# Attention scores of a hybrid decoder layer: products of 128, 64 and 3 rows, and the same with 128 rows throughout

## The chip, the cores and the metric

The kernel runs on one core of a Trainium2 chip. A core has a matrix engine (TensorE, PE in the profile), two engines for element-wise work (VectorE, DVE; ScalarE, ACT), GpSimd (POOL), which here issues the gathering DMAs, and SyncE (SP), which issues the other DMAs. The metric is the device time of one execution in microseconds (us), the median of several runs.

## What is computed

One layer over 1024 tokens of width 1024, in float32. The first half of the mixing width is retention, the second is differential attention with four heads; an expert layer follows. What the change touches is the attention score: each head has two maps of 64 query and key dimensions, and the output takes the first softmax less `lam` times the second.

```python
def diff_attention(q, k, v, lam):            # q,k: (B,T,H,2,d) with d = 64
    qb = (q * (d ** -0.5)).reshape(B, N, C, H, 2, d).transpose(1, 0, 3, 4, 2, 5)
    ...
    def block(args):
        qi, start = args
        ...
        bias = jnp.where(dist >= 0, -slopes[:, None, None] * dist, NEG_INF)
        s = jnp.einsum('bhpid,bhpjd->bhpij', qi, kt) + bias[None, :, None]
        p = jax.nn.softmax(s, axis=-1)
        a = p[:, :, 0] - lam * p[:, :, 1]
        return jnp.einsum('bhij,bhjv->bhiv', a, vt)
```

## The kernel before

Tokens go in eight tiles of 128. Three tiles are the sparse group (their experts are gathered row by row with indirect DMAs), five are the dense group (all experts are computed for them). `front` is a generator that yields the steps of the layer for one group; `weave` mixes the steps of two generators. The written order is not the final one: the framework orders the instructions of each engine by its own model of their times, and what a tile's room (its tag with `bufs` buffers) allows.

Numbers of high precision are kept as a high part, rounded to the fast float32r format, and a low part, the rest. A projection is three products (high by high, high by low, low by high), written in `mm` and shown in the profile as L160, L161, L162. `proj_t` makes a transposed projection into the bank `psT`; for the dense group in two halves of 320 tokens, for the sparse group in one of 384. Its bank has one room.

`att_proj(h)` prepares head h. The projection is evacuated into `pt` (one room). Of the queries, map m has a tile `q2[m]`: its own 64 rows hold the high part (L301, ScalarE), the other 64 rows the low part (L302, VectorE). Of the keys, `kd[m]` holds the high part twice (L316, L317), and `kl` holds the low parts of both maps (L318), so that one 128-row product of `q2[m]` and `kd[m]` gives high by high plus low by high, and a 64-row product of the high queries and `kl` adds high by low. The queries have two rooms per map, `kd` alternates between two places, `kl` has one room (`KL = 1`). The sparse group stores its keys in DRAM (`kd_d`), and the dense group loads them on GpSimd's queue (L309).

`attention(h)` takes the query tiles in turn. For each map and each 512 keys it starts with the linear bias, a product of 3 rows in bfloat16 (L342), adds the 128-row product (L344) and the 64-row product (L345), and in the block on the diagonal a mask (L347). VectorE takes the maximum (L350, L352), ScalarE the exponential (L356), VectorE the weighted difference (L361), TensorE transposes it (L368, `psA`) and multiplies it by the values (L372, `pov`). The steps of head h's attention are woven with its retention (`ret`, L272 to L283) and with the projections of head h + 1.

In the dense group's attention the gathered experts of the sparse tiles are already under way: GpSimd issues the gathers (L860), and VectorE forms their dot products (L862); `gated` opens the way for a fixed number of them after each step. After the attention come the output projection, the routing, the weight matrices of the dense tiles and the long loop over all experts.

Of the kernel before, what the change touches and what calls it, by code (L numbers as in the profile page):

```python
# [13 lines left out]
F32 = mybir.dt.float32  # L14
F32R = mybir.dt.float32r
# [8 lines left out]
P = 128  # L24
# [26 lines left out]
KL = 1  # L51
# [48 lines left out]
def layer_kernel(ctx, tc, x, wt, wn, wo, wq, sk, ut, u, v, gmix, gffn, gfin, gsub, dlam, consts, alb, out):  # L100
# [6 lines left out]
    kd_d = tc.dram_tile([H, 3, P, T], F32, name="kd_d")  # L107
# [25 lines left out]
    def front(m, pp, cst, g0, nt, dense, late):  # L133
        """Steps of the layer up to the routing for tiles g0..g0+nt, in the rooms m."""
# [13 lines left out]
        def chunk(src, shape):  # L148
            """Weights [128, k, m] in their hi and lo parts."""
# [48 lines left out]
        def split_t(src_of, name):  # L198
            """Transposes natural [128 t, 1024] tiles into [128, DC, n] operands."""
# [15 lines left out]
        # input norm  # L215
# [16 lines left out]
        # natural projections: rv, dv, rg  # L232
# [32 lines left out]
        def retention(h):  # L265
            qT, kT = ops[h][:2]
            for t in range(nt):
# [20 lines left out]
                jk = ap.tile([P, P], BF, tag="jk", bufs=2, name="jk")  # L288
# [5 lines left out]
        def att_proj(h):  # L294
            q2 = [ap.tile([P, n], F32R, tag=f"q2{m}", bufs=2, name=f"q2{m}") for m in range(2)]
            for a, b, ps in proj_t(wt[8 + 2 * h], hx):
                pt = ap.tile([P, b - a], F32, tag="pt", name="pt")
                A.activation(pt, ps, AF.Copy, scale=0.125)
                for m in range(2):
                    own, oth = slice(64 * m, 64 * m + 64), slice(64 - 64 * m, 128 - 64 * m)  # L300
                    A.activation(q2[m][own, a:b], pt[own], AF.Copy)  # L301
                    V.tensor_sub(q2[m][oth, a:b], pt[own], q2[m][own, a:b].bitcast(F32))  # L302
            yield
            kd2 = ap.tile([P, 2, L], F32R, tag="kd", name="kd") if h % 2 else fp.tile([P, 2, L], F32R, tag="R", name="kd")
            kd = [kd2[:, m] for m in range(2)]
            kl = ap.tile([P, L], F32R, tag="kl", bufs=KL, name="kl")
            if not first:
                for m, tl in enumerate(kd + [kl]):
                    G.dma_start(tl[:, :lo0], kd_d[h, m][:, :lo0])  # L309
            for a, b, ps in proj_t(wt[8 + 2 * h + 1], hx):  # L310
# [3 lines left out]
                for m in range(2):  # L314
                    own, oth = slice(64 * m, 64 * m + 64), slice(64 - 64 * m, 128 - 64 * m)
                    A.activation(kd[m][own, sl], pt[own], AF.Copy)  # L316
                    A.activation(kd[m][oth, sl], pt[own], AF.Copy)  # L317
                    V.tensor_sub(kl[own, sl], pt[own], kd[m][own, sl].bitcast(F32))  # L318
            if not last:
                for m, tl in enumerate(kd + [kl]):  # L320
                    SY.dma_start(kd_d[h, m][:, lo0:L], tl[:, lo0:].bitcast(F32))
            ops[h] += [q2, kd, kl]
            yield

        def attention(h):
            q2, kd, kl = ops[h][2:]
            dvh = ap.tile([P, g0 + nt, P], F32, tag="dvh", bufs=1, name="dvh")
            SY.dma_start(dvh, dv_d[:g0 + nt, :, h * P:(h + 1) * P].rearrange("t p c -> p t c"))
            for t in range(nt):
# [4 lines left out]
                for m in range(2):  # L334
                    pr = slice(m * 64, (m + 1) * 64)
                    ps = bankA("psS") if both is None else both[:, m:m + 1]
                    ql = slice(t * P, (t + 1) * P)
                    for b in range((Lq + 511) // 512):
# [5 lines left out]
                        PE.matmul(o, q2[m][:, ql], kd[m][:, c0:c1], start=False, stop=False)  # L344
                        PE.matmul(o, q2[m][pr, ql], kl[pr, c0:c1], start=False, stop=not diag)  # L345
# [27 lines left out]
                jk = ap.tile([P, P], BF, tag="jk", bufs=2, name="jk")  # L373
# [25 lines left out]
        # output projection and residual  # L399
# [34 lines left out]
        for hp in range(2 * PH):  # L434
# [4 lines left out]
            skt = fp.tile([P, NK], F32, tag="skt", bufs=1, name="skt")  # L439
# [33 lines left out]
    class Routed:  # L473
        """What the routing of a group leaves for later: key ranks and scores."""
# [8 lines left out]
    def decode(rp, late, t, eqs=("eq", 1), tmp=("tmp", 1), cs=("c2", 1)):  # L483
        """Key indices i1, i2 of tile t as [token, (head, rank)]."""
# [34 lines left out]
    def gates_of(rp, late, nt, tag):  # L519
        """Softmax of the scores of tiles 0..nt, in their place."""  # L520
# [9 lines left out]
    def sparse_routes(rp, late, g0, nt, *rooms):  # L530
        """Steps that leave expert indices and weights of the sparse tiles."""
# [9 lines left out]
    def dense_routes(rp, gp, pp, late):  # L541
        """Steps that put the weight matrices of the dense tiles into DRAM."""
# [22 lines left out]
    def build_g(gp, pp, r, lo, tb):  # L565
        """Weight matrices of one token tile: G[i2, i1, token] into DRAM."""
# [35 lines left out]
    def front_consts(cst, fp, wp):  # L602
# [47 lines left out]
    def weave(a, b, na=1, nb=1):  # L650
        """Steps of a and b in turn, nb of b to na of a."""
# [257 lines left out]
```

## Time and profile before

| what | value |
|---|---|
| time, median of 3 runs | 2943.44 us (2942.09 to 2951.27) |
| span of the profiled execution, its own time on the core | 2961.6 us |
| TensorE busy | 2799.5 us, 95% |
| VectorE busy | 2355.3 us, 80% |
| ScalarE busy | 1064.6 us, 36% |
| GpSimd busy | 1056.9 us, 36% |
| mean granted clock of TensorE over the span | 0.958 |

The profile gives the profiled execution's time only as its span, from the first to the last instruction; it is 18.2 us above the median of the three runs. Matmuls are pipelined: the duration of one reaches into the next, so what a product costs in a stream is read from the distance between two starts. The granted clock is 1.00 at 2.4 GHz and 0.50 at 1.2 GHz; a mean between them is a share of time at each.

### The profile page before, as it was taken

Reading aid. Unit: us, or ns where it says so; the run is one execution under the profiler, and the core shown is the slowest. Engines: PE = TensorE matmul, PEld = TensorE weight load, DVE = VectorE, ACT = ScalarE, POOL = GpSimd, SP = SyncE. Lnnn points to the kernel's source line nnn. Section 1 sums busy time; section 2 is a strip of 40 time slices with the busy share of each in tenths; the row PEclk is TensorE's granted clock in tenths of the full one; section 3 lists DMA queues with packets and bytes.
Section 4 is the critical chain, followed back from the end, with each engine's and each line's share of the span. In section 5 each row is a group of like instructions: output and inputs, shape, how many; then the busy total and the mean of one; then the engine's idle time right before and its main releaser. Section 6 shows DMA issues by size and latency. Waiting matters only on the chain.

```text
span 2961.6 us, 43054 instructions
## 1 busy us (share of the span) xinstructions
PE 2799.5 (95%) x16043; PEld 2478.4 (84%) x16043; DVE 2355.3 (80%) x4522; ACT 1064.6 (36%) x1882; POOL 1056.9 (36%) x786
## 2 busy tenths in 40 slices
PE   7989989998889999999989999999999999999998
PEld 6868877776679999998777788899989989999987
DVE  3455888756769999985777888888889988888988
ACT  4553334433333248996212222222322222222222
POOL 0000003423330000001545444566566666665554
PEclk9989998876989999999999999999999999999999
DMA  5334236744662226667888888899999999999997
GB/s 166 108 121 140 94 118 206 247 150 152 241 239 89 85 97 226 242 240 285 305 293 305 308 301 312 318 330 334 344 337 336 341 341 335 341 338 321 344 339 264
DMA packets 293956, 742.90 MB, mean 251 GB/s; under 512 B 23529, under 2 KB 118761, under 8 KB 293746
## 3 DMA queue, kind: packets, MB, share of 16 engines
q0 software_dynamic: 112320, 405.06, 38.8%
q1 hardware_dynamic: 181426, 335.09, 33.0%
q8 instruction: 125, 2.05, 0.3%
q14 instruction: 85, 0.70, 0.1%
HBM read 670.92 MB, written 69.14 MB: 250 GB/s over the span
## 4 chain that ended last, share of the span: by engine, by line
PE 35%; issue 27%; DMA 11%; DVE 9%; POOL 4%; ACT 1%; POOLq 0%; DVEq 0%; ACTq 0%
DMA gt<-g_d 5%; PE psH L722 4%; PE psH L721 4%; PE psH L720 4%; POOL vg L867 3%; DMA vg<-in_v,idx 3%; PE psV L794 3%; PE psV L795 3%; PE psV L796 3%; DMA gl<-hs_d 2%; DVE sa L869 2%; PE kp L795 2%; PE kp L794 2%; PE kp L796 2%; DVE vl L818 1%
## 5 line engine op out<-in xcount | busy, mean ns | idle before, releaser
L867 POOL DMA_INDIRECT vg<-in_v,idx x384 | 528.5, 1376 | 923.0 <-DVE ug L862 521.5
L860 POOL DMA_INDIRECT ug<-in_u,idx x384 | 520.9, 1356 | 522.1 <-DVE ug L862 370.7
L869 DVE SCALAR_TENSOR_TENSOR sa<-vg,shs,sa 128x1024 f32<-128x1024 f32 x384 | 492.4, 1282 | 42.3 <-DMA vg<-in_v,idx 38.7
L862 DVE SCALAR_TENSOR_TENSOR ug<-ug,sx 128x1024 f32<-128x1024 f32 x384 | 461.2, 1222 | 62.6 <-DMA ug<-in_u,idx 61.9
L720 PE MATMUL psH<-nh,uh 128*128 128x320 f32 x1424 | 439.7, 309 | 0.1
L721 PE MATMUL psH<-nl,uh 128*128 128x320 f32 x1424 | 439.6, 309 | 0.0
L722 PE MATMUL psH<-nh,ul 128*128 128x320 f32 x1424 | 438.7, 309 | 0.8 <-DVE ul L708 0.8
L794 PE MATMUL psV<-vh,wh 128*128 128x512 f32 x768 | 306.8, 401 | 36.3 <-DVE acc L830 35.8
L795 PE MATMUL psV<-vl,wh 128*128 128x512 f32 x768 | 305.0, 398 | 0.0
L796 PE MATMUL psV<-vh,wl 128*128 128x512 f32 x768 | 297.4, 396 | 0.0
L720 PEld LDWEIGHTS psH<-nh,uh 128*128 128x128 f32 x1424 | 267.5, 188 | 6.4 <-ACT uh L706 0.9
L721 PEld LDWEIGHTS psH<-nl,uh 128*128 128x128 f32 x1424 | 267.3, 188 | 5.2
L722 PEld LDWEIGHTS psH<-nh,ul 128*128 128x128 f32 x1424 | 267.1, 188 | 4.4 <-DVE ul L708 1.6
L723 ACT ACTIVATE ga<-psH 128x320 f32<-128x320 f32 x178 | 74.6, 426 | 438.4 <-PE psH L722 396.4
L706 ACT ACTIVATE uh<-uraw 128x1024 fp32r<-128x1024 f32 x128 | 135.7, 1060 | 209.7 <-PE psH L721 120.3
L794 PEld LDWEIGHTS psV<-vh,wh 128*128 128x128 f32 x768 | 147.9, 193 | 68.7 <-DVE acc L830 38.6
L720 PE MATMUL psHs<-nh,uh 128*128 128x320 f32 x624 | 196.3, 316 | 9.1 <-ACT ga L723 8.9
L153 ACT ACTIVATE whi<-wraw 128x1024 fp32r<-128x1024 f32 x104 | 110.1, 1059 | 258.4 <-PE psT L161 141.4
L155 DVE TENSOR_TENSOR wlo<-wraw,whi 128x1024 fp32r<-128x1024 f32 x104 | 126.9, 1220 | 94.6 <-ACT whi L153 92.3
L795 PE MATMUL kp<-vl,wh 128*128 128x512 f32 x512 | 199.2, 392 | 0.4 <-DVE vl L818 0.4
L794 PE MATMUL kp<-vh,wh 128*128 128x512 f32 x512 | 193.2, 393 | 4.7 <-ACT wh L810 4.7
L708 DVE TENSOR_TENSOR ul<-uraw,uh 128x1024 fp32r<-128x1024 f32 x128 | 156.4, 1222 | 48.7 <-ACT uh L706 48.6
(242 smaller groups left out, 6271.0 us busy)
## 6 DMA issues: line engine op xcount, KB each, us to landing
uraw<-in_ut SPq DMA_DIRECT2D x128, 512.0 KB, 6.3
vraw<-in_v SPq DMA_DIRECT2D x128, 512.0 KB, 6.9
g_d<-st SPq DMA_DIRECT2D x80, 512.0 KB, 4.7
gt<-g_d SPq DMA_DIRECT2D x32, 1280.0 KB, 18.0
wraw<-in_wt SPq DMA_DIRECT2D x32, 512.0 KB, 3.7
wraw<-in_wq SPq DMA_DIRECT2D x32, 512.0 KB, 3.8
hs_d<-ga SPq DMA_DIRECT2D x39, 320.0 KB, 2.6
gl<-hs_d SPq DMA_DIRECT2D x39, 320.0 KB, 5.9
```

What stands on the lines that cost most here:

```text
L706: A.activation(uh, raw, AF.Copy)
L708: V.tensor_sub(ul, raw, uh.bitcast(F32))
L720: PE.matmul(ps, uh[:, dc], xh[:, dc, sl], start=(dc == 0), stop=False)
L721: PE.matmul(ps, uh[:, dc], xl[:, dc, sl], start=False, stop=False)
L722: PE.matmul(ps, ul[:, dc], xh[:, dc, sl], start=False, stop=(dc == DC - 1))
L794: PE.matmul(ps, Wh[e][:, sl], Vh[e][:, so], start=start, stop=False)
L795: PE.matmul(ps, Wh[e][:, sl], Vl[e][:, so], start=False, stop=False)
L796: PE.matmul(ps, Wl[e][:, sl], Vh[e][:, so], start=False, stop=stop)
L860: G.indirect_dma_start(out=ug, out_offset=None, in_=u, in_offset=bass.IndirectOffsetOnAxis(ap=idxA[t][:, k:k + 1], axis=0))
L862: gate(V.scalar_tensor_tensor(ug, ug, 1.0, xt, op0=ALU.mult, op1=ALU.mult, accum_out=hs[:, k:k + 1]))
L867: G.indirect_dma_start(out=vg, out_offset=None, in_=v, in_offset=bass.IndirectOffsetOnAxis(ap=idxA[t][:, k:k + 1], axis=0))
L869: gate(V.scalar_tensor_tensor(ac, vg, hs[:, k:k + 1], ac, op0=ALU.mult, op1=ALU.add))
```

## The change

The keys become the operand with two halves, and the queries come twice. `kk[m]` holds the high part of map m's keys in the map's own 64 rows and the low part in the other 64. `qa[m]` holds the high part of the queries in both halves, `qb[m]` the low part in both halves. The product of `qa[m]` and `kk[m]` is high by high plus high by low, that of `qb[m]` and `kk[m]` low by high plus low by low; both have 128 rows. The bias operands have 128 rows, of which 125 are zero. `kl` is gone. Of the rooms, `qb` has one per map, the scratch tile `jk` one instead of two; `skt` and `cd` of the routing share the tags of other tiles and have two. In the profile of the changed kernel the lines after `UG` stand one or two away.

```diff
-KL = 1
...
-    kd_d = tc.dram_tile([H, 3, P, T], F32, name="kd_d")
+    kd_d = tc.dram_tile([H, 2, P, T], F32, name="kd_d")
...
-            q2 = [ap.tile([P, n], F32R, tag=f"q2{m}", bufs=2, name=f"q2{m}") for m in range(2)]
+            qa = [ap.tile([P, n], F32R, tag=f"q2{m}", bufs=2, name=f"qa{m}") for m in range(2)]
+            qb = [ap.tile([P, n], F32R, tag=f"qb{m}", bufs=1, name=f"qb{m}") for m in range(2)]
...
-                    A.activation(q2[m][own, a:b], pt[own], AF.Copy)
-                    V.tensor_sub(q2[m][oth, a:b], pt[own], q2[m][own, a:b].bitcast(F32))
+                    A.activation(qa[m][own, a:b], pt[own], AF.Copy)
+                    A.activation(qa[m][oth, a:b], pt[own], AF.Copy)
+                    V.tensor_sub(qb[m][own, a:b], pt[own], qa[m][own, a:b].bitcast(F32))
+                    V.tensor_sub(qb[m][oth, a:b], pt[own], qa[m][own, a:b].bitcast(F32))
...
-                    A.activation(kd[m][own, sl], pt[own], AF.Copy)
-                    A.activation(kd[m][oth, sl], pt[own], AF.Copy)
-                    V.tensor_sub(kl[own, sl], pt[own], kd[m][own, sl].bitcast(F32))
+                    A.activation(kk[m][own, sl], pt[own], AF.Copy)
+                    V.tensor_sub(kk[m][oth, sl], pt[own], kk[m][own, sl].bitcast(F32))
...
-                        PE.matmul(o, q2[m][:, ql], kd[m][:, c0:c1], start=False, stop=False)
-                        PE.matmul(o, q2[m][pr, ql], kl[pr, c0:c1], start=False, stop=not diag)
+                        PE.matmul(o, qa[m][:, ql], kk[m][:, c0:c1], start=False, stop=False)
+                        PE.matmul(o, qb[m][:, ql], kk[m][:, c0:c1], start=False, stop=not diag)
...
-            skt = fp.tile([P, NK], F32, tag="skt", bufs=1, name="skt")
+            skt = fp.tile([P, NK], F32, tag="at", bufs=2, name="skt")
...
-                cd = fp.tile([P, nt, NC2], F32, tag="kl", bufs=KL, name="cd")
+                cd = fp.tile([P, nt, NC2], F32, tag="q20", bufs=2, name="cd")
...
-        ab = fp.tile([3, H * P + T], BF, tag="ab", name="ab")
+        ab = fp.tile([P, H * P + T], BF, tag="ab", name="ab")
+        V.memset(ab, 0.0)
...
-            V.tensor_copy(ab[:, c0:c0 + 512], al)
+            V.tensor_copy(ab[:3, c0:c0 + 512], al)
```

The scheduler's order moves with it. On TensorE, before, the first score block of dense head 1 (queries `q_4174`, tile of 512 keys) stands right behind the value products and the retention of head 0:

```order
L372 MATMUL pov<-dvh,aT 128x128 x4
L279 MATMUL ret<-rv,am 128x128
L281 MATMUL ret<-S,qT 128x128
L342 LDWEIGHTS ab
L342 MATMUL psS<-ab 128x512
L344 MATMUL psS<-kd,q_4174 128x512
L345 MATMUL psS<-kl,q_4174 128x512
L347 LDWEIGHTS identb
L347 MATMUL psS<-maskb,identb 128x128
```

In the changed kernel the same place reads (the last row of the key projection first, `qa_4187` and `qb_4189` the queries of head 1):

```order
L161 MATMUL psT<-hh,wlo 128x320
L341 LDWEIGHTS ab
L341 MATMUL psS<-ab 128x512
L341 LDWEIGHTS ab
L341 MATMUL psS<-ab 128x512
L371 MATMUL pov<-dvh,aT 128x128 x3
L271 MATMUL ret<-qT,kT 128x128
L343 MATMUL psS<-kk,qa_4187 128x512
L344 MATMUL psS<-kk,qb_4189 128x512
L346 LDWEIGHTS identb
L346 MATMUL psS<-maskb,identb 128x128
```

The second half of head 1's key projection, which stood one projection earlier, is now the one just ahead of the scores, and two biases run ahead of the value products.

On VectorE, before, where head 0's last maxima are taken (L350), the low keys of head 1 wait for TensorE (the names in brackets are the semaphores waited for); its queries (`q_4174`, `q_4175`) were done nine rows earlier, waiting for ScalarE alone:

```order
L302 TENSOR_TENSOR q_4174<-pt,q_4174 64x320 [waits Activation_49]
L302 TENSOR_TENSOR q_4175<-pt,q_4175 64x320 [waits Activation_49]
...
L362 RECIPROCAL rz<-Z 128x1 [waits Activation_49]
L862 SCALAR_TENSOR_TENSOR ug,shs<-ug,sx 128x1024 [waits DMASW4_49,DVE_49]
L359 RECIPROCAL rz<-Z 128x1 [waits Activation_49]
L350 TENSOR_REDUCE Z<-psS 128x1 [waits PE_49]
L318 TENSOR_TENSOR kl<-pt,kd 64x320 [waits PE_49,Activation_49]
L318 TENSOR_TENSOR kl<-pt,kd 64x320 [waits Activation_49]
L350 TENSOR_REDUCE Z<-psS 128x1 [waits PE_49]
```

In the changed kernel the first half of head 1's queries stands there, and its keys only come some 20 rows later:

```order
L361 RECIPROCAL rz<-Z 128x1 [waits Activation_49]
L862 SCALAR_TENSOR_TENSOR ug,shs<-ug,sx 128x1024 [waits DMASW3_49,DVE_49]
L358 RECIPROCAL rz<-Z 128x1 [waits Activation_49]
L862 SCALAR_TENSOR_TENSOR ug,shs<-ug,sx 128x1024 [waits DMASW4_49,DVE_49]
L303 TENSOR_TENSOR qb_4189<-pt,qa_4187 64x320 [waits PE_49]
L304 TENSOR_TENSOR qb_4189<-pt,qa_4187 64x320
L349 TENSOR_REDUCE Z<-psS 128x1 [waits PE_49]
L303 TENSOR_TENSOR qb_4190<-pt,qa_4188 64x320 [waits PE_49]
L304 TENSOR_TENSOR qb_4190<-pt,qa_4188 64x320
L349 TENSOR_REDUCE Z<-psS 128x1 [waits PE_49]
...
L318 TENSOR_TENSOR kk<-pt,kk 64x320 [waits Activation_49] x2
```

The wait for the room moved from the keys to the queries, a projection earlier in the head. The number of gathers ahead of each milestone (the first dense expert, the routing, the output projection) is the same in both orders.

## Rows read from the trace of the kernel before

**Rows 1.** The page: busy time and share; clock in tenths by 40 slices.

```profile
PE 2799.5 (95%) x16043; PEld 2478.4 (84%) x16043; DVE 2355.3 (80%) x4522; ACT 1064.6 (36%) x1882; POOL 1056.9 (36%) x786
...
PEclk9989998876989999999999999999999999999999
```

**Rows 2.** Stretches (sparse, dense heads 0-3): length, PE, PEld, DVE, ACT, POOL busy, clock, DMA.

```profile
60.00:205.00 145.00, 131.32 (x697) 111.60 (x697) 62.29 (x123) 80.88 (x211) 0.00 (x0) 0.96 0.34 111
445.00:508.90 63.90, 62.38 (x314) 48.98 (x314) 52.62 (x102) 27.22 (x64) 22.05 (x19) 0.88 0.58 199
508.90:591.00 82.10, 77.95 (x407) 62.39 (x406) 62.55 (x109) 34.31 (x85) 40.33 (x35) 0.85 0.75 249
591.00:667.00 76.00, 72.93 (x316) 54.81 (x316) 43.89 (x81) 27.20 (x77) 21.75 (x21) 0.72 0.49 149
667.00:747.00 80.00, 71.64 (x283) 50.70 (x282) 48.05 (x90) 29.68 (x82) 26.30 (x22) 0.65 0.49 160
```

**Rows 3.** Waits, 445 to 747 us: us in total, times, longest.

```profile
DVE Z L350 <- PE psS L347: 34.0, 17, 4.1
DVE ug L862 <- DMA ug<-in_u,idx: 15.2, 13, 2.2
...
POOL kl L309 <- PE psS L347: 7.0, 1, 7.0
PE psA L368 <- DVE e L361: 5.6, 2, 4.1
```

**Rows 4.** Timeline of TensorE in a projection, products 1 and 4: start us, us.

```profile
35.50 0.39 PE L161 MATMUL psN<-wlo,hh 128*128 128x512 f32 x1
...
36.18 0.39 PE L161 MATMUL psN<-wlo,hh 128*128 128x512 f32 x1
```

**Rows 5.** Timeline of TensorE in score blocks at full clock, dense head 0.

```profile
503.08 0.38 PE L342 MATMUL psS<-ab 3*128 3x512 bf16 x1
503.39 0.50 PE L344 MATMUL psS<-kd,q 128*128 128x512 f32 x1
503.83 0.50 PE L345 MATMUL psS<-kl,q 64*128 64x512 f32 x1
504.26 0.39 PE L342 MATMUL psS<-ab 3*128 3x512 bf16 x1
...
505.44 0.23 PE L347 MATMUL psS<-maskb,identb 128*128 128x128 bf16 x1
505.60 0.38 PE L342 MATMUL psS<-ab 3*128 3x512 bf16 x1
```

**Rows 6.** Timeline of TensorE at half clock: two projection products, a score block.

```profile
510.59 0.47 PE L160 MATMUL psT<-hh,whi 128*128 128x320 f32 x1
510.86 0.47 PE L161 MATMUL psT<-hl,whi 128*128 128x320 f32 x1
...
525.80 0.60 PE L342 MATMUL psS<-ab 3*128 3x512 bf16 x1
...
528.00 0.60 PE L342 MATMUL psS<-ab 3*128 3x512 bf16 x1
```

**Rows 7.** Timeline of TensorE in a masked block of 256 columns, sparse head 0.

```profile
85.36 0.28 PE L342 MATMUL psS<-ab 3*128 3x256 bf16 x1
...
86.20 0.23 PE L347 MATMUL psS<-maskb,identb 128*128 128x128 bf16 x1
```

**Rows 8.** Weight loads to 760 us: shape, count | busy us, mean ns | idle before.

```profile
L161 PEld LDWEIGHTS psN<-wlo,hh 128*128 128x128 f32 x163 | 31.3, 192 | 8.4 <-DVE wlo L155 2.6
...
L342 PEld LDWEIGHTS <-ab 3*128 3x128 bf16 x96 | 8.7, 93 | 18.9 <-issue 14.8 <-PE psT L161 0.5 <-PE psS L347 0.2
```

**Rows 9.** Line 345 by itself: duration ns min/median/max, first and last start, forms.

```profile
L345 PE MATMUL psS<-kl,q x96: 322/492/792, 83.7 to 745.0; 64*128 64x512 f32 x48, 64*128 64x128 f32 x16, 64*128 64x256 f32 x16, 64*128 64x384 f32 x16
```

**Rows 10.** Groups of VectorE, 60 to 760 us.

```profile
L302 DVE TENSOR_TENSOR q<-pt,q 64x320 fp32r<-64x320 f32 (+1 forms) x24 | 12.2, 508 | 0.7
L862 DVE SCALAR_TENSOR_TENSOR ug<-ug,sx 128x1024 f32<-128x1024 f32 x91 | 109.4, 1220 | 17.1 <-DMA ug<-in_u,idx 16.7
```

More of the change, by code (lines that the diff above doesn't have):

```diff
@@ L287, in retention @@
                         V.tensor_copy(S[:, h], bank[:, 3])
-                jk = ap.tile([P, P], BF, tag="jk", bufs=2, name="jk")
+                jk = ap.tile([P, P], BF, tag="jk", bufs=1, name="jk")
                 A.activation(jk, bank[:, 2], AF.Square, scale=cst["cross"][:, h:h + 1],
@@ L300, in att_proj @@
                     own, oth = slice(64 * m, 64 * m + 64), slice(64 - 64 * m, 128 - 64 * m)
-                    A.activation(q2[m][own, a:b], pt[own], AF.Copy)
-                    V.tensor_sub(q2[m][oth, a:b], pt[own], q2[m][own, a:b].bitcast(F32))
+                    A.activation(qa[m][own, a:b], pt[own], AF.Copy)
+                    A.activation(qa[m][oth, a:b], pt[own], AF.Copy)
+                    V.tensor_sub(qb[m][own, a:b], pt[own], qa[m][own, a:b].bitcast(F32))
+                    V.tensor_sub(qb[m][oth, a:b], pt[own], qa[m][own, a:b].bitcast(F32))
             yield
-            kd2 = ap.tile([P, 2, L], F32R, tag="kd", name="kd") if h % 2 else fp.tile([P, 2, L], F32R, tag="R", name="kd")
-            kd = [kd2[:, m] for m in range(2)]
-            kl = ap.tile([P, L], F32R, tag="kl", bufs=KL, name="kl")
+            kk2 = ap.tile([P, 2, L], F32R, tag="kd", name="kk") if h % 2 else fp.tile([P, 2, L], F32R, tag="R", name="kk")
+            kk = [kk2[:, m] for m in range(2)]
             if not first:
-                for m, tl in enumerate(kd + [kl]):
+                for m, tl in enumerate(kk):
                     G.dma_start(tl[:, :lo0], kd_d[h, m][:, :lo0])
@@ L315, in att_proj @@
                     own, oth = slice(64 * m, 64 * m + 64), slice(64 - 64 * m, 128 - 64 * m)
-                    A.activation(kd[m][own, sl], pt[own], AF.Copy)
-                    A.activation(kd[m][oth, sl], pt[own], AF.Copy)
-                    V.tensor_sub(kl[own, sl], pt[own], kd[m][own, sl].bitcast(F32))
+                    A.activation(kk[m][own, sl], pt[own], AF.Copy)
+                    V.tensor_sub(kk[m][oth, sl], pt[own], kk[m][own, sl].bitcast(F32))
             if not last:
-                for m, tl in enumerate(kd + [kl]):
+                for m, tl in enumerate(kk):
                     SY.dma_start(kd_d[h, m][:, lo0:L], tl[:, lo0:].bitcast(F32))
-            ops[h] += [q2, kd, kl]
+            ops[h] += [qa, qb, kk]
             yield
         def attention(h):
-            q2, kd, kl = ops[h][2:]
+            qa, qb, kk = ops[h][2:]
             dvh = ap.tile([P, g0 + nt, P], F32, tag="dvh", bufs=1, name="dvh")
@@ L334, in attention @@
                 for m in range(2):
-                    pr = slice(m * 64, (m + 1) * 64)
                     ps = bankA("psS") if both is None else both[:, m:m + 1]
@@ L372, in attention @@
                     PE.matmul(po[:, :P], aT[:, b], dvh[:, b], start=(b == 0), stop=(b == tg))
-                jk = ap.tile([P, P], BF, tag="jk", bufs=2, name="jk")
+                jk = ap.tile([P, P], BF, tag="jk", bufs=1, name="jk")
                 A.activation(jk, po[:, :P], AF.Square, scale=rz[:, 0:1], accum_out=msd[:, t, h:h + 1])
```

## The prediction

> **What bounds the kernel now.** I read the page first. TensorE is counted busy for 95% of the span, and its granted clock is full or nearly so except in the third, the seventh to tenth and the twelfth of the 40 slices of 74 us [rows 1]; the seventh to tenth, 444 to 740 us, hold the attention of the five dense tiles. The view of busy time by stretch, cut at the last score matmul of each head, gives the stages that the change touches [rows 2]: the three sparse tiles (145 us) and dense heads 0, 1, 2, 3 (63.9, 82.1, 76.0, 80.0 us). TensorE is busy 90 to 98% of each. VectorE is the next, and very unequal: 62.3 of 145 us in the sparse stretch, 52.6 of 63.9 and 62.6 of 82.1 in dense heads 0 and 1, 43.9 of 76.0 and 48.1 of 80.0 in heads 2 and 3. The table of waits of the dense stretch says who is late [rows 3]: VectorE stood 34.0 us for score tiles, while TensorE stood only 5.6 us for the weighted difference of the exponentials. So TensorE is the bound of this stage, with VectorE close behind in heads 0 and 1. What comes after the attention keeps its instructions and its number of gathered experts per step, so I take its length as fixed, and what the stage gives up the kernel gives up.
>
> **What a change of row count costs.** The timeline shows it by the starts of neighbours. A plain 128-row product of 512 columns starts 0.227 us after its like (35.50 to 36.18 in three steps), although each loads weights for 0.19 us [rows 4, 8]: the load is hidden. In a score block at full clock [rows 5] the 3-row bias takes 0.31 us to the next start, the 128-row product before the 64-row one 0.44, the 64-row one 0.43; going back to 3 rows costs again: the 128-column mask product takes 0.16 us to the next bias (505.44 to 505.60) where its columns are worth 0.06, a quarter of 0.227. A 512-column block is 1.18 us without the mask (503.08 to 504.26) and 1.34 with it (504.26 to 505.60), against 3 x 0.227 = 0.68 and 0.74 of columns. At half clock [rows 6] the masked block is 2.20 us (525.80 to 528.00), and a 320-column product takes 0.267 (510.59 to 510.86), so 512 columns 0.427 and the masked block 3 x 0.427 + 0.08 = 1.36 without switches: 0.84 us lost to them instead of 0.60.
>
> **What the change removes.** Afterwards all four kinds of product have 128 rows. A 128-row bf16 bias is nowhere in the trace; with 512 columns it lies between 0.227 us (the f32r product of as many) and the 0.31 of the 3-row bias, and I take the former, because the rest of the 0.31 is the switch; the latter would cost 6 us. Narrow blocks are bounded by columns below and by a weight load of 0.19 us above [rows 8]; a 256-column masked block takes 0.84 + 0.16 = 1.00 us (85.36 to 86.20, and the mask) [rows 7], afterwards, with a product at 0.16 between these bounds (0.11 and 0.19), 3 x 0.16 + 0.07 = 0.55, a gain of 0.45. The gain of a 384-column block I put between its neighbours at 0.50, that of a 128-column one below at 0.30, since the weight load keeps it from shrinking with the columns. Of the 96 blocks 48 have 512 columns, 32 of them unmasked, and 16 each have 384, 256, 128 [rows 9]. At full clock: 32 x 0.50 + 16 x (0.60 + 0.50 + 0.45 + 0.30) = 16.0 + 29.6 = 45.6 us, which is 2.5 us for a sparse head and 8.9 for a dense one. The clock in the four dense heads is 0.88, 0.85, 0.72, 0.65, so 24, 30, 56 and 70% of their time is at half clock [rows 2]; with 0.84/0.60 = 1.4 times the loss there, the dense heads give 9.8, 10.0, 10.9, 11.4 us and the sparse ones 10.3: **52 us of TensorE time**.
>
> **The clock.** Within dense head 0 the blocks stand 1.18 and 1.34 us apart at 2.4 GHz, and one tile of scores later they run at 1.2 GHz whole [rows 5, 6]; the engine had gone through a tile's four blocks with their switches in between. Half clock takes 2 x (1 - 0.88) x 63.9 and so on: 15 + 25 + 43 + 56 = 139 us of the dense heads. If none were left it would be worth up to half of that again; the floor of VectorE limits it. I take 2, 3, 6 and 6 us for the four heads, a guess at a quarter.
>
> **What the change adds.** Evacuating a query projection goes from one subtraction per map and half to two: 24 more on VectorE at 0.508 us [rows 10], 12.2 us in all, 2 per dense head; ScalarE gets 24 copies for queries and loses 24 for keys, all of one shape. The clearing of the bias tile is one VectorE instruction of 128 x 768 at the very start, ahead of the first input. Four stores and four loads of the low keys go; one of those loads held GpSimd's queue for 7.0 us behind a score block [rows 3]. The second room for the subkeys and for the candidates lies in the routing, where TensorE is bound by projections: nothing.
>
> The costly part is the single room of the low queries. By the order on VectorE, the queries of head 1 now wait for the last score blocks of head 0, and with them the evacuation tile `pt`, the bank of the projection, and the key projection. The low keys had the same single room, so the wait moves one step ahead and is not of a new kind. What waits now: the key projection (2 x 24 products of 320 columns, 0.14 us each by 320/512 of 0.227, 7 us) comes after the last scores, with transposes and value products beside it, and the first scores of the next head come behind two more evacuations on a VectorE that has gathered experts (1.22 us each [rows 10]) in between. In the sparse stretch there are no gathers: I take 1 us for each of three changes of head, in the dense 2 to 3 us.
>
> **The sum by stage.** Sparse: 145 - 10.3 + 3 gives 7. Head 0: the floor is VectorE's 52.6 + 2 = 54.6 of 63.9, so at most 9; an order in which both engines wait for each other never reaches it, I take 5. Head 1: floor 64.6 of 82.1, TensorE 10.0 + 3 - 3: 10. Head 2: 10.9 + 6 - 3: 14. Head 3, with no next head: 11.4 + 6, less 3 for the chain through VectorE: 14. Together 50 us. The profiled execution spans 2961.6 us, 18.2 over the median of the three runs, 2943.44; no stage of it that I use is in question, and 50 us is the same in both within half a us. Forecast: 2943.4 - 50 = **2893 us**. Other orders of the same instructions in the later dense loop may move it by some 5 us either way.
>
> **Rivals.** (1) *VectorE eats half.* Its 207 of the 302 us of the dense heads [rows 2], its gathers and its in-order queue become the bound in all of them; 20 to 30 us are left: 2918. For it: heads 0 and 1 stand at 82 and 76% of VectorE, and it stood 15.2 us for gathers [rows 3]. Against: heads 2 and 3 at 58 and 60%. (2) *The clock comes back whole.* Then heads 2 and 3 go toward VectorE's 46 and 50 us: 9 for the sparse stretch, 9, 15, 25 and 25 for the heads, 83 us, 2860. For it: the low clock lies where the switching blocks lie. Against: heads 2 and 3 also have fewer projections to stream. (3) *The weight loads show.* If a product with the row count of its predecessor had to wait for its own load, a 512-column block would take 3 x 0.227 + 0.09 + 2 x 0.19 = 1.15 us against 1.18, and the change would give 3 us: 2940. Against: the projections, equal in rows, step by 0.227 with loads of 0.19 [rows 4, 8]. The Trainium skill (TensorE: Matmul & The Clock Gate, Part 3: Packing small matmuls — row/col tiling) says that a weight load overlaps a running product only when their row groups differ. By that rule 128 rows everywhere would lose the overlap and the time would be this rival's 2940; the trace disagrees, since the products with equal rows are the ones that step without a gap (0.227 us). (4) *Slower: the single room.* Per change of dense head the chain after the last score is four subtractions, an evacuation, half a projection of 3.5 us, an evacuation, two copies, two subtractions, and the second half with the same again, with some eight gathered experts of 1.2 us between on VectorE: 20 to 25 us. TensorE has some 12 us of work of its own for that time. Were that work queued behind the waiting products, the stall would be 20 to 25 us at three changes and 3 us at three sparse ones, 69 to 84 us, against the 59 us that the sum above holds before its stalls (50 + 9): 10 to 25 us slower, 2960. It decides from 17 us of stall per dense change. For it: one engine queue in order, and a wait of this kind in [rows 3] already (GpSimd 7.0 us for the low keys' room). Against: in the order on TensorE the projections and value products stand ahead of the next head's scores, not behind them.
>
> **How the numbers follow.** Forecast (2875 to 2908) 0.50; rival 1, stalls of rival 4 short of a loss among it (2908 to 2932), 0.24; rival 2 (2850 to 2875) 0.16; rival 3 0.03, no change for another reason 0.02; rival 4 0.05. 0.3% of the time is 8.8 us, about what a measurement can tell. Faster by more 0.90, same 0.05, slower 0.05. The range 2860 to 2927 leaves out the far 0.06 of rival 2, 0.05 of rival 1, and rivals 3 and 4 with the other no-change case: 2 in 10. The forecast's own range is 2875 to 2908.
>
> **What would show it.** Right: a 512-column block at full clock starts its successor after 0.68 us (0.75 masked), no idle of weight loads before score products; VectorE's 34.0 us of waiting for scores falls to under 20; clock in heads 2 and 3 above 0.75; dense heads of about 59, 72, 62 and 66 us. Wrong: block starts unchanged (rival 3), TensorE idle before the first scores of each head (rival 4), VectorE over 90% busy in all heads (rival 1). If the stages shrink and the span does not, my premise on the later stages fails.

## The result, and the profile after

The changed kernel takes 2906.35 us (median of 4 runs, 2900.81 to 2909.91) against 2943.28 for before in the same comparison: 0.9865 of its time, 95% interval 0.9846 to 0.9883, 37 us less. A second comparison, with 6 runs of after and 11 of before, gave 2905.83 against 2951.03: 0.9845 (0.982 to 0.987), 45 us less. The forecast was 2893 us, 50 us less, in a range of 2860 to 2927.

The page of the kernel after, busy time and granted clock, beside [rows 1]:

```profile
PE 2712.1 (94%) x16043; PEld 2441.4 (84%) x16043; DVE 2363.5 (82%) x4547; ACT 1063.9 (37%) x1881; POOL 1047.4 (36%) x782
...
PEclk9989998999989999999999999999999999999999
```

The digits to compare are the seventh to tenth of the clock: 8, 9, 9, 9 where before has 8, 8, 7, 6. TensorE is busy 87 us less, VectorE 8 us more. The stretches of the kernel after, with the columns of [rows 2]: the window of the sparse tiles, dense heads 0 to 3 cut at their last score product, the four heads together, and what lies between the last score product and the first expert:

```profile
60.00:205.00 145.00, 125.08 (x732) 111.17 (x731) 73.61 (x157) 85.61 (x228) 0.00 (x0) 0.95 0.35 116
441.50:488.50 47.00, 41.76 (x262) 36.27 (x261) 44.13 (x81) 20.77 (x51) 23.90 (x20) 0.93 0.74 251
488.50:559.10 70.60, 61.12 (x393) 54.94 (x392) 60.28 (x110) 34.10 (x90) 33.99 (x30) 0.93 0.75 256
559.10:628.50 69.40, 59.25 (x393) 53.45 (x393) 53.10 (x95) 32.27 (x81) 25.18 (x22) 0.93 0.61 200
628.50:682.70 54.20, 42.01 (x243) 33.82 (x242) 45.98 (x91) 28.18 (x81) 25.00 (x20) 0.87 0.60 199
441.50:682.70 241.20, 204.14 (x1285) 178.48 (x1285) 203.49 (x375) 115.32 (x303) 108.06 (x91) 0.92 0.67 226
682.70:811.10 128.40, 105.36 (x487) 85.65 (x487) 92.70 (x174) 41.52 (x78) 45.87 (x38) 0.92 0.73 256
```

Heads 2 and 3, at a clock of 0.72 and 0.65 in [rows 2], are now at 0.93 and 0.87; the last score product starts at 682.7 us instead of 745.7. TensorE was busy 90 to 98% of each stretch before; now it is busy 204 of 241 us, 85%, and VectorE 203 of 241, 84%: neither engine is full. By head VectorE is busy 94, 85, 77 and 85% of the time.

TensorE's timeline in a masked pair of 512-column blocks at full clock, dense head 3 (start, duration, line; the bias is now L341, the two key products L343 and L344, the mask L346), beside [rows 5]:

```profile
679.34 0.38 PE L341 MATMUL psS<-ab 128*128 128x512 bf16 x1
679.37 0.58 PE L343 MATMUL psS<-kk,qa 128*128 128x512 f32 x1
679.78 0.40 PE L344 MATMUL psS<-kk,qb 128*128 128x512 f32 x1
680.02 0.39 PE L341 MATMUL psS<-ab 128*128 128x512 bf16 x1
680.06 0.58 PE L343 MATMUL psS<-kk,qa 128*128 128x512 f32 x1
680.48 0.40 PE L344 MATMUL psS<-kk,qb 128*128 128x512 f32 x1
680.72 0.23 PE L346 MATMUL psS<-maskb,identb 128*128 128x128 bf16 x1
680.79 0.66 PE L371 MATMUL pov<-dvh,aT 128*128 128x128 f32 x4
```

The unmasked block takes 0.68 us (679.34 to 680.02), the masked one 0.77 (680.02 to 680.79). The steps inside a block, 0.03, 0.41 and 0.24, are not equal; only their sum can be compared with three products of 0.227 us.

Waits in the dense heads of the kernel after, 441 to 683 us, beside [rows 3]:

```profile
DVE ug L862 <- DMA ug<-in_u,idx: 22.8, 15, 4.1
...
PE psA L367 <- DVE e L360: 10.5, 7, 3.6
...
PE psT L159 <- ACT pt L298: 8.0, 2, 5.5
...
ACT pt L298 <- DVE qb L304: 7.3, 2, 4.4
...
DVE Z L349 <- PE psS L346: 3.0, 4, 1.5
```

VectorE's wait for scores fell from 34.0 to 3.0 us. In its place TensorE waits: 10.5 us for the weighted difference (5.6 before), and 8.0 us before a projection for the query evacuation, which itself stood 7.3 us behind the subtractions into `qb`. VectorE was not idle before any of these subtractions in the dense heads (32 ns at most): it had other work ahead of them in its order. VectorE's own longest wait is for gathered rows, 22.8 us (15.2 before).

### The profile page after: what moved, and what is told of

Its sections match the earlier page's. It is cut to its first block, busy times and chain, and to the rows that moved or that the text cites. A ratio compares the mean times of both kernels' runs of the same rounds, so it can differ in the third digit from the quotient of the medians.

```text
span 2899.0 us, 43071 instructions
## 1 busy us (share of the span) xinstructions
PE 2712.1 (94%) x16043; PEld 2441.4 (84%) x16043; DVE 2363.5 (82%) x4547; ACT 1063.9 (37%) x1881; POOL 1047.4 (36%) x782
## 4 chain that ended last, share of the span: by engine, by line
PE 46%; DVE 14%; DMA 10%; issue 9%; POOL 3%; ACT 3%; SPq 0%; POOLq 0%; DVEq 0%; ACTq 0%
PE psH L721 6%; PE psH L722 6%; PE psH L720 6%; DMA gt<-g_d 4%; PE psV L794 4%; PE psV L795 3%; PE psV L796 3%; DMA ug<-in_u,idx 2%; PE kp L795 2%; PE kp L796 2%; PE kp L794 2%; PE psHs L720 2%; PE psHs L722 2%; DVE sa L869 2%; PE psHs L721 2%
## 5 line engine op out<-in xcount | busy, mean ns | idle before, releaser
L860 POOL DMA_INDIRECT ug<-in_u,idx x384 | 511.9, 1333 | 502.7 <-DVE ug L862 335.4
L721 PE MATMUL psHs<-nl,uh 128*128 128x320 f32 x624 | 195.1, 313 | 0.0
```

Of the source, the lines that this page charges most:

```text
L721: PE.matmul(ps, uh[:, dc], xl[:, dc, sl], start=False, stop=False)
L860: G.indirect_dma_start(out=ug, out_offset=None, in_=u, in_offset=bass.IndirectOffsetOnAxis(ap=idxA[t][:, k:k + 1], axis=0))
```

## The experiments

**Theory.** The gain is the row counts: the time lost at changes of row count in the score blocks goes, and with it most of the half clock; what the new operands add (24 subtractions, a single room) costs part of it. Rivals: the clock came back through another order of the instructions, since the planner may lay the program anew after an edit; VectorE eats part of the gain; the single room does. Comparisons of one group share one chip and the runs of before. What is said below of the order of the instructions compares the traces of TensorE, VectorE, ScalarE and GpSimd, instruction by instruction, by operation, tile name and shape; buffer numbers are not in them.

**Before once more** (no edit).

> The kernel before, unchanged, for a second profile and for the clock of each run. The profiled execution of before spans 2961.6 us, 18 over the median of its runs; 62.6 us lie between the two profiled spans, 37 between the medians. Theory: the surplus is half clock in the dense heads, which differs from execution to execution. Then this profile spans 2940 to 2952, its last score product ends near 727 to 735 instead of 745.7, and the half clock between 445 and that point is 100 to 120 us instead of 139. Rival: the surplus lies in the expert loops, and the attention ends at 745 again.

2952.86 us (10 runs, 2943.15 to 2970.16), ratio 1.0002. Its dense heads, from the first masked score product of head 0 to the last of head 3:

```profile
451.70:738.00 286.30, 268.61 (x1282) 203.45 (x1281) 199.03 (x361) 114.91 (x302) 110.78 (x95) 0.80 0.60 196
```

Half clock is 2 x (1 - 0.80) x 286.3 = 115 us here. In the first profile it was 2 x (1 - 0.77) x 294.0 = 135. The attention ends 7.7 us earlier than there and the span is 10 us shorter: most of the surplus of the first profile lies in the dense heads and goes with their clock, as the theory has it, though the last score product at 738 is later than expected. This profile is the one that after is compared with below.

**The bias alone, before's other products kept:**

```diff
-        ab = fp.tile([3, H * P + T], BF, tag="ab", name="ab")
+        ab = fp.tile([P, H * P + T], BF, tag="ab", name="ab")
+        V.memset(ab, 0.0)
...
-            V.tensor_copy(ab[:, c0:c0 + 512], al)
+            V.tensor_copy(ab[:3, c0:c0 + 512], al)
```

> Before, with the bias operand padded to 128 rows and nothing else; the 64-row product of low keys stays. Theory (each change of row count has its own price): the 3-row bias costs 0.31 us to its successor against 0.227 for 128 rows, and coming back to it after the 128-row mask costs 0.095, so a masked 512-column block goes from 1.34 to 1.16 us and an unmasked one from 1.18 to 1.09: 32 x 0.09 + 64 x 0.18 = 14 us at full clock, some 16 with the half-clock share, so about 2927 (2920 to 2935). The 0.43 us from 128 to 64 rows and the 0.43 from 64 on stay. Rival 1 (the drain comes once per block, however many row counts differ): 2943. Rival 2 (the row counts pull the clock down, and the bias is enough of it): the clock of dense heads 2 and 3 rises from 0.72 and 0.65 to 0.85 or more, and the time falls to 2915 or lower.

2918.12 us, ratio 0.9873 (0.985 to 0.9897). Its dense heads:

```profile
447.10:701.30 254.20, 222.13 (x1283) 176.98 (x1282) 197.06 (x360) 115.09 (x304) 114.22 (x95) 0.93 0.67 219
```

The starts of the bias products there (unmasked block, then masked):

```profile
491.05 0.38 PE L342 MATMUL psS<-ab 128*128 128x512 bf16 x1
...
492.01 0.39 PE L342 MATMUL psS<-ab 128*128 128x512 bf16 x1
...
493.06 0.38 PE L342 MATMUL psS<-ab 128*128 128x512 bf16 x1
```

The blocks are 0.96 and 1.05 us, 0.22 and 0.29 less than in before: more than the expected 0.09 and 0.18. The clock goes from 0.80 to 0.93, half clock from 115 to 36 us. Rival 2 of this run is right on the clock (0.92 and 0.85 in heads 2 and 3) and, nearly, on the time.

This run also bears on the order. But for the clearing of the tile its order is that of before on all four engines, up to TensorE's 2789th product, which lies early in head 2; from there on it differs in places. The stretch from the first masked score product of head 0 to that point, first in before and then here:

```profile
451.70:600.20 148.50, 142.53 (x736) 113.08 (x736) 116.56 (x208) 64.39 (x160) 66.90 (x58) 0.86 0.70 231
...
447.10:578.60 131.50, 120.27 (x737) 100.21 (x737) 113.12 (x205) 63.88 (x159) 69.96 (x58) 0.97 0.76 254
```

In an unchanged order, with the bias alone on 128 rows, the clock goes from 0.86 to 0.97 and the stretch is 17 us shorter.

**After with the bias back at a 3-row tile** (the diff above reversed, in after).

> After, with the bias back at 3 rows and nothing else. Theory: each of the 96 blocks gets 0.09 us going to the bias and 0.09 leaving it, 17 us of TensorE, of which what lies in the sparse stretch and in heads 0 and 1, some 10 us, and most of the rest shows: 2920 (2914 to 2926). Rival (TensorE is no more the bound in the dense heads, since it stands for VectorE): only the sparse share of 5 us shows, 2906 to 2911.

2919.06 us, ratio 0.9881 (0.9859 to 0.9903), as the theory expects (2914 to 2926); against 0.9845 for after it is some 11 us more. The order on the four engines is after's up to the last tile of head 3, but for the clearing of the bias tile on VectorE, which is not there.

**After with two rooms for the low queries:**

```diff
...
-            qb = [ap.tile([P, n], F32R, tag=f"qb{m}", bufs=1, name=f"qb{m}") for m in range(2)]
+            spare = late.spare() if h % 2 else None
+            qb = [spare[:, m] if h % 2 else
+                  ap.tile([P, n], F32R, tag=f"qb{m}", bufs=1, name=f"qb{m}") for m in range(2)]
...
```

The low queries of odd heads lie in the room of the routing's results, which opens for these only after the attention.

> After, with a second room for the low queries: those of odd heads lie in the room of the routing's results, which are first written after the attention. Theory: TensorE stands 5.5 us and 2.5 us before the query projection for the evacuation tile, which waits for the subtraction into the single room; with two rooms these gaps go and the time falls by 5 to 10 us: 2899 (2894 to 2903). Rival (what TensorE gains there it waits elsewhere for VectorE, which is busy 84% of the dense heads): 2903 to 2909, no change that can be told.

2925.65 us, ratio 0.9909 (0.9885 to 0.9932): slower than after, and outside both the theory and the rival. TensorE's waits in its dense heads, 438 to 690 us:

```profile
PE psA L369 <- DVE e L362: 20.8, 10, 4.8
...
PE psT L159 <- ACT pt L300: 2.7, 1, 2.7
```

The wait for the evacuation falls from 8.0 to 2.7 us, and the wait for the weighted difference rises from 10.5 to 20.8. The stall moved to the next thing that VectorE owes TensorE; the expected gain is absent. The dense heads, and the stretch from there to the first expert:

```profile
438.80:683.10 244.30, 201.00 (x1263) 175.84 (x1262) 201.04 (x371) 114.07 (x296) 111.36 (x89) 0.92 0.66 219
683.10:832.60 149.50, 113.08 (x508) 91.15 (x508) 96.13 (x184) 43.34 (x85) 47.87 (x40) 0.89 0.66 226
```

The heads take 244.3 us against 241.2 in after. This kernel is slower than after by 0.0064 of before's time, 19 us, and most of that lies behind the heads: 149.5 us to the first expert against 128.4. What makes that stretch longer was not isolated; the order is another from the sparse tiles on, and the edit moves the opening of the routing's room.

**The bias of 64 rows, and of 3, in after's order.** The 64-row kernel has on all engines the same instructions in the same order as after; the 3-row one up to the last tile of head 3, and it has throughout the order of the kernel with the 3-row tile above, but for the clearing. The rows left out are zeros.

```diff
-                        PE.matmul(o, cst["albl"][:, h], cst["albr"][:, rl:rl + c1 - c0], start=True, stop=False)
+                        PE.matmul(o, cst["albl"][:64, h], cst["albr"][:64, rl:rl + c1 - c0], start=True, stop=False)
```

> The kernel after, unchanged, beside runs of before on one chip, with a second profile. Before has shown 2952.9 as the median of ten runs in the second measurement instead of 2943. Theory: the whole change is then worth more than the 37 us of the first comparison, since its profiles gain 55 us against the second profile of before (738.0 to 682.7 at the last score product): ratio 0.983 to 0.986, 2902 to 2912 where before is 2952. The last score product at 680 to 690 us, 30 to 50 us of half clock in the dense heads. Rival: 0.9865 to 0.990, and the 55 us are given back in the expert loops.

> After, with the bias product reading 64 of its 128 rows (the others are zeros); the order of all instructions on every engine is the same as after's, word for word. By the spacing in before, going from 128 to 64 rows costs 0.21 us and back 0.20: 96 x 0.41 = 39 us of TensorE, about as much as all row counts of before cost (46 us). Theory A (the switches pull the clock down, and the clock was the greater part of the gain): the half clock in the dense heads goes from 41 to over 90 us, and with the switches the time rises to 2950 (2940 to 2965). Theory B (the clock came back through another order of the instructions): half clock stays at 30 to 55 us, the sparse stretch gets 9 us longer and the dense heads 10 to 20, since TensorE stands 15% of them: 2925 to 2937. Theory C (VectorE bounds the dense heads): only the sparse 9 us, 2912 to 2920.

> After, with the bias product reading 3 of its 128 rows; up to the last tile of head 3 the order on every engine is that of after. The price is 0.09 us going to 3 rows and 0.09 back, 96 x 0.18 = 17 us of TensorE, 5 in the sparse stretch and 3 in each dense head. Theory A: half clock in the dense heads between that of after and that of the 64-row bias, 2925 to 2940. Theory B: half clock 30 to 55 us, 2912 to 2922. Theory C: 2908 to 2913. The kernel with a 3-row tile, in another order, had 2919 beside before at 2955.

After, repeated: 2905.83, ratio 0.9845, last score product at 684.6 us. With 64 rows 2915.02, 0.9875 (0.985 to 0.9901); with 3 rows 2919.05, 0.9891 (0.9863 to 0.9919), the time of the kernel with the 3-row tile (2919.06). The dense heads of the 64-row kernel:

```profile
443.40:691.10 247.70, 219.48 (x1284) 176.22 (x1283) 206.14 (x382) 115.13 (x303) 107.35 (x92) 0.94 0.67 221
```

A block of it:

```profile
559.63 0.39 PE L341 MATMUL psS<-ab 64*128 64x512 bf16 x1
559.95 0.50 PE L343 MATMUL psS<-kk,qa 128*128 128x512 f32 x1
560.29 0.40 PE L344 MATMUL psS<-kk,qb 128*128 128x512 f32 x1
560.62 0.39 PE L341 MATMUL psS<-ab 64*128 64x512 bf16 x1
```

The block is 0.99 us, 0.31 more than after's; with 3 rows it is 0.98 to 0.99. Over 72 blocks of the dense heads that is at most some 22 us of TensorE (an estimate, with 0.30 for blocks of every width). Its busy time rises by 15.3 us (204.14 to 219.48), its idle time falls by 8.8, and the stage gets 6.5 us longer, with the clock at 0.94. Theory A falls: bias switches alone do not bring the half clock back. The time of the 64-row kernel is theory C's, that of the 3-row kernel theory B's; the stages lie between the two, since the dense heads do get longer, but more than half of the switches' cost there goes into time in which TensorE waits anyway. The expected prices, 39 and 17 us, were both wrong: it is some 28 for either (an estimate, 96 blocks at up to 0.30).

**Before with all products on 128 rows and nothing else:** the padded bias, and the other map's rows let into the low-key product, where they add the product of this map's low queries and the other map's low keys. That product is no part of the score; the expectation takes it to be smaller than the scores' rounding, which no run here measures.

```diff
-                        PE.matmul(o, q2[m][pr, ql], kl[pr, c0:c1], start=False, stop=not diag)
+                        PE.matmul(o, q2[m][:, ql], kl[:, c0:c1], start=False, stop=not diag)
```

> Before, with the bias padded to 128 rows and the product of the low keys on all 128 rows: the key tile holds the low halves of both maps, so the other map's 64 rows add a product of two low halves, smaller than the rounding of the scores. All products have 128 rows as in after, but without the 24 subtractions, the copies of queries and the single room of low queries. Theory (the gain is row counts and clock, the rest of the change only costs): as fast as after or faster by up to 8 us, 2895 to 2910 where before is 2952. Rival (the arrangement of the operands itself is worth something, through other waits): slower than after by more than 5 us.

2886.55 us, ratio 0.9787 (0.9762 to 0.9812): 19 us faster than after on the same chip, and below the expected 2895 to 2910. Its dense heads:

```profile
438.20:674.40 236.20, 202.49 (x1272) 175.34 (x1281) 196.89 (x363) 115.32 (x303) 118.47 (x95) 0.93 0.72 235
```

**Before's row counts with the padded tile, and the low-key product alone on 128 rows.** The first is the padded bias of above with the product reading `[:3]`; the second is the last diff by itself.

> Before with the bias tile padded and cleared, but its product reading 3 rows: the row counts of before (3, 128, 64, 128) in an order of the instructions that the planner laid anew. Theory A (the row counts together cost the time and hold the clock down): 2951 (2943 to 2960), dense heads 280 to 295 us with over 100 us of half clock. Theory B (the low clock of before came from the order of its instructions, and any other order gives some of it back): 2920 to 2935, dense heads of 255 to 270 us, half clock under 70.

> Before with the low-key product on all 128 rows and the bias on 3 (the other map's 64 rows add a product of two low halves). The order is nearly that of before. Theory A: as in after with a 3-row bias, a block pays 0.30 us for the bias, 28 us of TensorE, of which 10 to 13 showed there; so 2886.6 and 13, 2900 (2894 to 2908), half clock 30 to 50 us in the dense heads. Theory B: the order of before keeps over 100 us of half clock, and the time is 2920 or more.

2953.36 us, ratio 1.0016 (0.9996 to 1.0035), and 2904.63 us, ratio 0.985 (0.9829 to 0.9871). Their dense heads:

```profile
451.80:740.00 288.20, 269.25 (x1283) 206.49 (x1283) 199.22 (x361) 115.24 (x303) 114.00 (x95) 0.80 0.59 194
```

```profile
441.90:674.10 232.20, 209.69 (x1274) 168.41 (x1274) 194.54 (x354) 114.53 (x298) 109.68 (x92) 0.98 0.71 235
```

The first was meant to have another order. Its trace has before's: TensorE, ScalarE and GpSimd run the same instructions in the same order throughout, and VectorE has one more, the clearing of the tile. So it says nothing of other orders; it shows that padding and clearing by themselves change neither the time nor the clock, and that it is the rows read by the product that count. With the same tile and 128 rows read the clock was 0.97 up to head 2, in the same order; here it is 0.87:

```profile
451.80:601.40 149.60, 141.52 (x736) 113.49 (x736) 117.01 (x209) 64.72 (x161) 70.24 (x58) 0.87 0.69 230
```

The second kernel's order leaves before's in the first sparse tile. Its time is theory A's. Its clock is 0.98 in the dense heads, 9 us of half clock where theory A has 30 to 50; but between them and the first expert it is 0.89, and that stretch takes 137.0 us against 121.5 with all rows at 128:

```profile
674.10:811.10 137.00, 109.35 (x497) 88.26 (x496) 94.47 (x179) 43.28 (x85) 50.46 (x39) 0.89 0.69 243
```

The low clock goes with the row counts in an order that is held fixed, so another order is not needed to explain its return; whether new orders add to it was not measured. The starts of the bias products around one unmasked block, for the padded tile read at 3 rows, the low-key product alone on 128, and all on 128:

```profile
503.21 0.38 PE L342 MATMUL psS<-ab 3*128 3x512 bf16 x1
504.38 0.38 PE L342 MATMUL psS<-ab 3*128 3x512 bf16 x1
...
487.20 0.39 PE L342 MATMUL psS<-ab 3*128 3x512 bf16 x1
488.19 0.38 PE L342 MATMUL psS<-ab 3*128 3x512 bf16 x1
...
482.44 0.38 PE L342 MATMUL psS<-ab 128*128 128x512 bf16 x1
483.13 0.39 PE L342 MATMUL psS<-ab 128*128 128x512 bf16 x1
```

The four kernels without new operands make a table (half clock is 2 x (1 - clock) x length; the block is an unmasked one of 512 columns):

| rows of bias, of low product | block, us | dense heads, us | TensorE busy | half clock, us | time to before |
|---|---|---|---|---|---|
| 3, 64, padded tile, before's order | 1.17 | 288.2 | 269.3 | 115 | 1.0016 |
| 128, 64 | 0.96 | 254.2 | 222.1 | 36 | 0.9873 |
| 3, 128 | 0.98 | 232.2 | 209.7 | 9 | 0.985 |
| 128, 128 | 0.68 | 236.2 | 202.5 | 33 | 0.9787 |
| after: 128, 128, new operands | 0.68 | 241.2 | 204.1 | 39 | 0.9845 |

**After with the other half of the low queries cleared once** and not written again: 24 subtractions fewer, and the product of the two low halves left out.

```diff
...
+                    V.memset(keep["qb"][m][64 - 64 * m:128 - 64 * m].bitcast(F32), 0.0)
...
-                    V.tensor_sub(qb[m][oth, a:b], pt[own], qa[m][own, a:b].bitcast(F32))
```

> After, with the other half of the low-query tiles cleared once for a group of tiles and not written again: 24 subtractions fewer on VectorE (12 us; 8 of them in the dense heads, 4 us), rooms as in after. The product of the two low halves, which before does not have either, falls away. After is 19 us slower than the kernel that makes all products 128 rows without new tiles (2886.6). Theory D (the added subtractions are what this costs): 2890 to 2897. Theory E (it is the single room of the low queries and the order around it): 2902 to 2908.

2911.01 us, ratio 0.9872 (0.985 to 0.9893): no gain, so theory D is not borne out; theory E's 2902 to 2908 is missed too. The order is another than after's from the sparse tiles on, so a gain of a few us could be hidden.

**After with fewer gathered experts beside the attention** (`PER = (1.0, 1.0, 0.0)` in place of 1.5).

> After, with one gathered expert opened for each step of the attention in place of one and a half; the rest are gathered later, so that only the stage is read, not the total. Theory (VectorE, busy 84% of the dense heads, is what TensorE stands for there, so part of the gain is eaten): a third of some 90 gathered experts of 1.22 us, 37 us of VectorE, goes, and the dense heads fall from 241 to 215 to 228 us with TensorE busy over 90%. Rival (the chains between the engines, not the load, hold it): 236 to 242 us. The total may go either way, 2890 to 2930.

Its dense heads:

```profile
441.90:657.50 215.60, 193.19 (x1279) 169.16 (x1279) 173.87 (x321) 114.43 (x297) 78.64 (x64) 0.97 0.57 190
```

The dense heads fall to 215.6 us, with TensorE busy for 90% of them; the total is 2958.87, over the expected 2890 to 2930, as the gathered experts are caught up later: from the first expert to the end it takes 2174.3 us against 2087.9. With 27 fewer gathers VectorE is busy 29.6 us less in the dense heads, its waits for gathered rows fall from 22.8 to 11.3 us, and the stage is 25.6 us shorter: what VectorE has to do and to wait for there holds the dense heads of after. The work and the waits are not told apart, and the clock rises with them, from 0.92 to 0.97.

## Why the prediction was right, point by point

**Row counts: right.** 0.68 us was forecast and measured for the unmasked block, 0.75 and 0.77 for the masked one. The weight loads do not show, so rival 3 is out: products with equal rows step without a gap, 0.68 us for three, and it is the change of rows that costs. The Trainium skill (TensorE: Matmul & The Clock Gate, Part 3: Packing small matmuls — row/col tiling) says that a weight load overlaps a running product only when the row groups differ, though it also names a load into a background weight buffer; the traces here do not bear out the first as a general rule. The mask products of the sparse tiles span 77.7 us (85.8 to 163.5), 88.7 before (84.0 to 172.7): 11.0 us less, where 10.3 were forecast for TensorE; as the first starts 1.8 us later, the last comes 9.2 us earlier, against 7 in the forecast's sum.

**Clock: right mechanism, too small a term.** The guess of 17 us was a quarter of what a full return could give. Half clock in the dense heads went from 115 us to 39, two thirds. TensorE's busy time there fell from 268.6 to 204.1, 64.5 us; with the forecast's 42 us for the switches, 22 remain for the clock (an estimate, since the two are not measured apart). The table shows that neither row count alone keeps the clock low; before's two together do. Rival 2, a whole return, did not come: 0.93, 0.93, 0.93 and 0.87 by head.

**Stalls: near in size, wrong place.** Dense heads: forecast 59 us of TensorE less 16 of stalls, 43; measured 64.5 less 19.4 of idle time more (17.7 to 37.1), 45. Against the first profile, from which the forecast was made, it is 294.0 to 241.2 us, 53: the forecast held that no stage of that profile was in question, and its dense heads were 7.7 us longer than in the second. The forecast placed the stalls mostly in the chain around the single room. The waits show 8.0 us there; a second room brought them to 2.7 and the dense heads got no shorter, while fewer gathered experts shortened them by 25.6 us. So the bound that took the rest is VectorE, the mechanism of rival 1, but at about the size that the forecast had for stalls; rival 1's price, by which only 20 to 30 us are left, did not come. By rival 1's own sign, VectorE busy over 90%, it holds in head 0 alone. Rival 4 did not come: 5.5 us is the longest wait before a projection.

**Heads: off one by one.** Forecast 72, 62 and 66 us for heads 1 to 3; measured 70.6, 69.4 and 54.2. Head 0, by one cut of both profiles, goes from 57.2 us (451.7 to 508.9) to 47.0, 10 us where 5 were forecast. Heads 2 and 3 together are 123.6 against 128; the cut at a last score product says little of which work lies on which side, when the order is new.

**Later stages: nearly fixed.** From the first expert to the end the profile takes 2087.9 us, 2090.0 in before's second profile. Between the last score product and the first expert after takes 128.4 against 123.5. In the repeat of after the two are 2092.9 and 129.5, so the second is longer than before's in both profiles.

**The sum, and where it was lucky.** The repeat of after (span 2907.0) and the second profile of before (2951.5) differ by 44.5 us, as the medians of the second comparison do. The first masked score product of head 0 comes 7.7 us earlier (451.7 to 444.0), the dense heads are 45.7 us shorter (286.3 to 240.6), and the two later stretches are 6.0 and 2.9 us longer. So the stages that were priced gave 53 us, 3 more than the forecast's 50, and the stages taken as fixed took 9 back. That the total comes out near the forecast is in part the luck of errors against each other.

**What the forecast did not see** is that the row counts can be had without the new arrangement of operands, which only costs. Row counts alone give 0.9787; the arrangement gives back 17 to 19 us. With a 3-row bias the same pair of kernels stands at 0.9891 and 0.985. Of the 16 us between their profiles 3 lie ahead of the dense heads, 5 in them (241.2 against 236.2, VectorE 6.6 us more busy) and 7 between them and the first expert (128.4 against 121.5). Neither the run without the subtractions nor the run with the second room returned it; both have other orders than after, and both edits together were not tried, so what the arrangement costs, and how much of it is the order, stays open.

## What to carry to other kernels

Price a change of row count from the spacing inside the whole block, before against after, and expect the prices not to add: about 0.30 us for either of two kinds of switch here, 0.50 for both. When the bound engine gets faster, sum its busy time and the idle time it will find behind the next engine separately; here 64.5 us of work bought 45. Before new operands are built to make shapes equal, look whether the rows at hand can be let into the product without new work: that version is 19 us faster, and the fastest of all kernels run here. Its price is a small product in the scores that does not belong there. And before a difference is put down to a new order, compare the orders in the traces: two of the kernels here that were taken for reordered were not.

## What the runs showed of the hardware

- A switch to 3 rows costs the same as one to 64: with either bias a block of 512 columns takes 0.98 to 0.99 us instead of 0.68. The Trainium skill (TensorEngine Tiling (Array Packing), Key Properties) says that changing the tiling mode drains TensorE; these runs agree in that the change costs time, and give the price, 0.30 us to go and come back once per block, where 64-row and 3-row products side by side need 0.50 for their three changes.
- Before's own time wanders with the clock: ten runs go from 2943.15 us at a mean clock of 0.968 to 2970.16 at 0.957. Six runs of after stay within 2900.5 and 2908.8, at 0.974 to 0.977. After scatters less than before. After's medians in the two comparisons are 0.5 us apart, before's 8: that is the difference between 37 and 45 us.
